# Stores of what ScalarE has just copied are begun by ScalarE in place of SyncE

## The chip, the core and the metric

The kernel runs on one core of a Trainium2 chip. The metric is the device time of one execution in microseconds (us). The engines are named as in the profile: PE is TensorE (its weight loads are shown as PEld), DVE is VectorE, ACT is ScalarE, POOL is GpSimd, SP is SyncE, which computes nothing and begins DMA transfers. SPq and ACTq are the DMA starts that SP and ACT execute. Each engine works off its own instruction list in order; they wait for each other through semaphores, and the DMA engines move data once a start has been executed.

## What is computed

One backbone layer over 512 latent tokens and 256 context tokens of width 2048, in 32-bit floats: an adaLN-modulated RMS norm, one input projection, two groups of heads that read it, a gate for each group, one output projection and a residual.

```python
def _project(xn, w_in, mu_shift):
    p = jnp.einsum('bld,de->ble', xn, w_in)
    sh, z_r, q, k, v, z_a = jnp.split(p, cuts, axis=-1)
    return _centred_shift(sh, mu_shift), z_r, q, k, v, z_a   # sh: r, k, v and two low-rank parts

def step(S, inp):                       # group A: RWKV-7 scan, both directions, 16 heads of 64
    r_t, w_t, k_t, v_t, kk_t, a_t = inp
    s_kk = jnp.einsum('bhvk,bhk->bhv', S, kk_t)
    S = (S * w_t[:, :, None, :] - s_kk[..., None] * (kk_t * a_t)[:, :, None, :]
         + v_t[..., None] * k_t[:, :, None, :])
    return S, jnp.einsum('bhvk,bhk->bhv', S, r_t)

# group B: 16 query heads on 4 key heads of 64, norm and rotary of q and k, a window of +-128
# latent tokens and all context keys in one softmax with a sink logit
# out = x + gate * (concat(y_A * silu(z_r), y_B * silu(z_a)) @ w_out)
```

## The kernel before

All matrices lie transposed: the 128 partitions are columns of the projection, the free axis is time (512 latent, then 256 context). Products in full precision are made of three with rounded halves: a weight tile from memory (`wf`) is cast by ACT to its high part (`whi`), DVE subtracts to get the low part (`wlo`), and PE multiplies high by high, high by low and low by high (`xh`, `xl` are the halves of the activations).

The 60 tiles of 128 projected columns come in kinds (`COLS`): `k`, `v`, `r` and the low-rank `lwa`, which are shifted in time, and `ak`, `av`, `q`, `zr`, `za`, which are not. The stages, by time in the trace:

- 0 to 225 us, `lockstep`: the modulation, the norm, and the first column tiles in step with the loads.
- 225 to 625: the other tiles that have context columns, beside the 8 context units of the RWKV scan.
- 625 to 1225: the tiles with latent columns only, beside 16 latent units (`unit`). Inside a unit small tiles (`it`, `iw`, `nb`) go through memory to change their layout.
- 1225 to 1362: `norms`, 12 items of norm and rotary for keys and queries (`norm_rope`), beside the last `za` tiles.
- 1362 to 1625: attention, with three quarters of the output projection beside it.
- 1625 to 1676: the last quarter; each of its 16 tiles ends in `finish`.

Four places write to memory what the next stages read. `evac` (line 988) takes a projected tile out of the accumulator: for unshifted kinds ACT copies it into `sh` and a store writes it to `dzr`, `dza`, `dq`, `dak` or `dav` (line 1031); for `k` and `r` DVE works last and the same line stores to `dk` or `dr`; for `v` PE turns it, ACT copies the turned rows back, and they are stored to `dvt` (line 1024), in two stores for a tile, latent and context. `norm_rope` ends in an ACT copy into `w`, stored to `dkf` or `dqf` (line 1468). `finish` ends in an ACT copy into `x`, stored to the output (line 735).

The order of the instructions is not that of the code. `Program` records every operation with what it reads and writes, and `order` (line 432) makes a list schedule: it keeps a clock for each engine and takes the ready operation with the longest chain of work behind it, where projection and output products and their evacuation are filler that other work precedes. Its prices for a DMA start depend on the engine: on SP a start holds the engine 450 or 625 ns and the transfers queue one behind the other, by size; on ACT it holds the engine 400 ns and what reads the result is ready 2000 ns later. `run` then emits each engine's list in that order, all from one line, which is why every row of the trace carries L500. A tile's buffer numbers are left out in the trace; tiles of different use share a buffer, so a row such as `kv<-psum` in the last stage is the `x` of `finish` in the buffer `kv`.

Of the kernel before, what the change touches and what calls it, by code (L numbers as in the profile page):

```python
# [60 lines left out]
MU_KINDS = ("lwa", "k", "v", "r")  # L61
# [451 lines left out]
class Body:  # L513
# [209 lines left out]
    def finish(self, j, acc, part):  # L723
        nc, a = self.nc, self.a
        fill, nc.fill = nc.fill, False
        y = self.t(self.wk, (128, 2, L), "fin")
        o, x = y[:, 0], y[:, 1]
        nc.sync.dma_start(out=x, in_=a["xt"][j][:, 0:L])
        nc.vector.tensor_tensor(o, acc, part, ALU.add)
        nc.vector.scalar_tensor_tensor(o, o, self.gcol[:, j:j + 1], x, ALU.mult, ALU.add)  # L730
        pt = self.t(self.pq, (128, 512), "pt", bufs=2)
        for t in range(4):
            nc.tensor.transpose(pt[:, 128 * t:128 * t + 128], o[:, 128 * t:128 * t + 128], self.ident)
        nc.scalar.copy(x, pt)
        nc.sync.dma_start(out=self.out[0].rearrange("(t p) c -> p t c", t=4)[:, :, 128 * j:128 * j + 128],
                          in_=x.rearrange("p (t c) -> p t c", t=4))
        nc.fill = fill

# [249 lines left out]
    def evac(self, j, pl, pc, o=None, banks=None):  # L988
        nc = self.nc
        kind, i, _ = COLS[j]  # L990
        segs = [(pl, 0, L)] + ([(pc, L, C)] if pc is not None else [])
        if o is None:
            o = (self.t(self.lp, (128, T), "lo", bufs=2) if kind == "lwa" else
                 self.t(self.stage, (128, T if j < NCTX else L), "sh", bufs=self.nsh))
        if kind in MU_KINDS:
            m = sum(1 for k, _, _ in COLS[:j] if k in MU_KINDS)
            om, hm = self.omm[:, m:m + 1], self.hmu[:, m:m + 1]
            for p, s, n in segs:
                nc.scalar.activation(o[:, s:s + n], p, AF.Identity, scale=om)
                nc.vector.scalar_tensor_tensor(o[:, s + 1:s + n], p[:, 0:n - 1], hm, o[:, s + 1:s + n], ALU.mult,  # L1000
                                               ALU.add)
                nc.vector.scalar_tensor_tensor(o[:, s:s + n - 1], p[:, 1:n], hm, o[:, s:s + n - 1], ALU.mult,
                                               ALU.add)
        else:
            for p, s, n in segs:
                nc.scalar.copy(o[:, s:s + n], p)
        if kind == "lwa":
            nc.scalar.activation(o[0:64, :], o[0:64, :], AF.Tanh)
            nc.sync.dma_start(out=self.dlw[i], in_=o)
            for m in range(2):  # L1010
                w = self.t(self.lp, (128, T), "lw", bufs=4)
                for h in range(2):
                    nc.sync.dma_start(out=w[64 * h:64 * h + 64], in_=self.dlw[i][64 * m:64 * m + 64])
                for st, sl in zip(self.lws[i][m], (slice(0, L), slice(L, T))):
                    nc.scalar.copy(st, w[:, sl])
                    nc.vector.tensor_tensor(st[64:128], w[64:128, sl], st[64:128].bitcast(F32), ALU.subtract)
            return
        if kind == "v":
            fill, nc.fill = nc.fill, False
            for p, (s, n) in zip(banks or (pl, pc), ((0, L), (L, C))):  # L1020
                for t in range(0, n, 128):
                    nc.tensor.transpose(p[:, t:t + 128], o[:, s + t:s + t + 128], self.ident)
                nc.scalar.copy(o[:, s:s + n], p[:, :n])
                nc.sync.dma_start(out=self.dvt[i][s:s + n].rearrange("(t q) c -> q t c", q=128),
                                  in_=o[:, s:s + n].rearrange("q (t c) -> q t c", c=128))
            nc.fill = fill
            return
        dst = {"k": self.dk, "ak": self.dak, "av": self.dav, "q": self.dq, "r": self.dr,
               "zr": self.dzr, "za": self.dza}[kind][i]
        n = T if pc is not None else L  # L1030
        nc.sync.dma_start(out=dst, in_=o[:, :n])

# [394 lines left out]
    def norm_rope(self, src, dst, tab, n, tiles, small, ps):  # L1429

        nc = self.nc
        ntt = n // 128
        x, w = (y[:, :n] for y in tiles())
        hd = lambda y: y.rearrange("p (t h c) -> p t h c", h=2, c=64)
        turn = lambda nm: self.t(ps, (128, 512), "pt", nm=nm)[:, :n]
        bc = lambda y: y.rearrange("p (t c) -> p t c", c=64).unsqueeze(2).to_broadcast([128, ntt, 2, 64])

        def turned(y, nm):
            p = turn(nm)
            for t in range(ntt):  # L1440
                nc.tensor.transpose(p[:, 128 * t:128 * t + 128], y[:, 128 * t:128 * t + 128], self.ident)
            return p

        nc.sync.dma_start(out=x, in_=src)
        pn = turned(x, "nn")
        nc.scalar.copy(x, pn)
        nc.scalar.activation(w, x, AF.Square)
        ms, *yw = (small[:, 8 * i:8 * i + 2 * ntt] for i in range(3))
        nc.vector.tensor_reduce(ms, w.rearrange("p (m c) -> p m c", c=64), AX.X, ALU.add)
        nc.vector.tensor_scalar(ms, ms, 1.0 / 64, 1e-6, ALU.mult, ALU.add)  # L1450
        inv = self.rsqrt(None, ms, 2 * ntt, yw)
        nc.vector.tensor_tensor(x.rearrange("p (m c) -> p m c", c=64), x.rearrange("p (m c) -> p m c", c=64),
                                inv.unsqueeze(2).to_broadcast([128, 2 * ntt, 64]), ALU.mult)
        if n == L:
            v = lambda y: y.rearrange("p (t h b s c) -> p t h b s c", h=2, b=2, s=2, c=16)
            sin = tab[1].rearrange("p (t b s c) -> p t b s c", b=2, s=2, c=16)
            for b in range(2):
                for q in range(2):
                    nc.vector.tensor_tensor(v(w)[:, :, :, b, q], v(x)[:, :, :, b, 1 - q],
                                            sin[:, :, b, q].unsqueeze(2).to_broadcast([128, ntt, 2, 16]), ALU.mult)  # L1460
            nc.gpsimd.tensor_tensor(hd(x), hd(x), bc(tab[0]), ALU.mult)
            nc.gpsimd.tensor_tensor(x, x, w, ALU.add)
        else:
            nc.gpsimd.tensor_tensor(hd(x), hd(x),
                                    tab[2].unsqueeze(1).unsqueeze(1).to_broadcast([128, ntt, 2, 64]), ALU.mult)
        pk = turned(x, "nk")
        nc.scalar.copy(w, pk)
        nc.sync.dma_start(out=dst, in_=w)

    def norms(self, wk, ps):  # L1470

# [242 lines left out]
```

## Time and profile before

| | before |
|---|---|
| three runs | 1673.76, 1680.74, 1681.35 us (median 1680.74) |
| profiled execution | 1677.45 us, its span 1675.6 us |
| busy share of the span | PE 93%, PEld 72%, DVE 79%, ACT 43%, POOL 24% |
| mean granted TensorE clock | 0.98 |
| DMA moved | 225.78 MB |
| DMA starts | SP 927, ACT 144 |

The span goes from the first to the last instruction of the execution. "Busy" is the time in which an engine executes; in a row of waits, `A x <- B y: total, times, longest` says that A stood still before writing x until B had written y. The DMA starts are counted in the instruction lists.

### The profile page before, as it was taken

The page shows a single profiled execution, that of the slowest core. Times are in us where ns is not written, and L with a number is a line of the kernel's source. Part 1 is how long each engine was busy: PE and PEld are TensorE (multiplying, and loading weights), DVE is VectorE, ACT ScalarE, POOL GpSimd, SP SyncE. Part 2 cuts the span into 40 slices and gives each one's busy share as a digit, 9 for nine tenths or more (in the row PEclk, how much of TensorE's full clock was granted, in tenths as well). Part 3 has the DMA queues.
Part 4 walks back from the last instruction along what each step waited for, and adds up shares of the span by engine and source line. Part 5 has one row for each costly group of instructions (what it writes and reads, how often), then busy time and mean ns, then how long its engine had stood idle before and what let it go on. Part 6 is the DMA issues. An engine that isn't in the chain of part 4 may idle for free. (4 is left out here: it accounts for less than half of the span.)

```text
span 1675.6 us, 34264 instructions
## 1 busy us (share of the span) xinstructions
PE 1556.3 (93%) x12454; PEld 1210.9 (72%) x12454; DVE 1319.0 (79%) x3921; ACT 716.6 (43%) x1484; POOL 404.0 (24%) x615
## 2 busy tenths in 40 slices
PE   7998898999999999999998898989888999999998
PEld 5666677878787777777666666767666778788887
DVE  2356889888898846989888898888889558899865
ACT  3432364333343333434443433434333338776723
POOL 2358613010111002122222323123234300111000
PEclk9999998999999999999999999999999999999999
DMA  9976464435444443333333233323343562222146
GB/s 352 332 244 227 123 196 150 129 100 148 118 145 141 139 129 125 116 89 114 107 107 100 92 106 98 100 87 111 89 133 118 170 189 76 76 70 70 45 132 195
DMA packets 215322, 225.78 MB, mean 135 GB/s; under 512 B 78704, under 2 KB 139632, under 8 KB 215152
## 3 DMA queue, kind: packets, MB, share of 16 engines
q1 hardware_dynamic: 181360, 218.86, 41.0%
q10 hardware_dynamic: 33792, 4.73, 1.7%
q8 instruction: 98, 1.61, 0.4%
q14 instruction: 72, 0.59, 0.1%
HBM read 190.49 MB, written 33.03 MB: 133 GB/s over the span
## 5 line engine op out<-in xcount | busy, mean ns | idle before, releaser
L500 PE MATMUL psum<-xh,whi.0_41_283 128*128 128x512 f32 x624 | 242.5, 412 | 1.7 <-DVE xh L500 1.1
L500 PE MATMUL psum<-xh,whi.1_44_313 128*128 128x512 f32 x624 | 240.0, 407 | 0.2 <-ACT xh L500 0.2
L500 PE MATMUL psum<-xh,wlo.0_42_287 128*128 128x512 f32 x528 | 216.3, 410 | 0.0
L500 PE MATMUL psum<-xh,wlo.1_45_325 128*128 128x512 f32 x528 | 215.2, 408 | 0.7 <-DVE wlo.1_45_325 L500 0.7
L500 PE MATMUL psum<-xl,whi.1_44_313 128*128 128x512 f32 x432 | 177.3, 411 | 4.4 <-DVE xl L500 4.4
L500 PE MATMUL psum<-xl,whi.0_41_283 128*128 128x512 f32 x432 | 177.9, 412 | 2.3 <-DVE xl L500 2.2
L500 DVE TENSOR_TENSOR s<-x,nb 128x60 f32<-128x60 f32 (+21 forms) x648 | 156.8, 242 | 10.1
L500 DVE TENSOR_TENSOR x<-x,s 128x60 f32<-128x60 f32 (+21 forms) x648 | 155.6, 240 | 10.6
L500 PEld LDWEIGHTS psum<-xh,whi.0_41_283 128*128 128x128 f32 x624 | 119.0, 192 | 29.6 <-issue 4.1
L500 PEld LDWEIGHTS psum<-xh,whi.1_44_313 128*128 128x128 f32 x624 | 117.8, 190 | 24.7 <-issue 2.9
L500 PEld LDWEIGHTS psum<-xh,wlo.0_42_287 128*128 128x128 f32 x528 | 101.3, 192 | 22.4 <-issue 1.6
L500 PEld LDWEIGHTS psum<-xh,wlo.1_45_325 128*128 128x128 f32 x528 | 100.5, 190 | 22.4 <-DVE wlo.1_45_325 L500 1.5
L500 PEld LDWEIGHTS psum<-xl,whi.0_41_283 128*128 128x128 f32 x432 | 83.4, 193 | 21.4 <-DVE xl L500 4.0
L500 PEld LDWEIGHTS psum<-xl,whi.1_44_313 128*128 128x128 f32 x432 | 82.4, 191 | 22.4 <-DVE xl L500 5.7
L500 ACT COPY uv<-psum 64x128 f32<-64x128 f32 (+2 forms) x103 | 29.1, 282 | 135.0 <-DVE uv L500 70.0
L500 PE MATMUL psum<-kr,bk 64*128 64x128 f32 (+1 forms) x640 | 67.0, 298 | 13.4 <-DVE x L500 4.5
L500 ACT ACTIVATE e<-psum,drv 128x256 f32<-128x256 f32 x96 | 44.4, 476 | 78.5 <-PE psum L500 23.1
L500 PEld LDWEIGHTS psum<-kr,bk 64*128 64x128 f32 (+1 forms) x640 | 54.0, 195 | 29.6 <-issue 10.1
L500 PE MATMUL psum<-uv,ar 64*64 64x64 f32 (+1 forms) x1280 | 71.2, 234 | 1.4 <-ACT uv L500 1.4
L500 PE MATMUL psum<-uv,kb 128*64 128x64 f32 (+1 forms) x848 | 64.9, 244 | 8.0 <-DVE uv L500 7.5
L500 PEld LDWEIGHTS psum<-uv,kb 128*64 128x64 f32 (+1 forms) x848 | 46.8, 141 | 32.5 <-DVE uv L500 13.9
L500 POOL TENSOR_TENSOR s<-s 128x128 f32<-128x128 f32 x56 | 34.8, 622 | 139.8 <-DVE s L500 111.8
(376 smaller groups left out, 3828.2 us busy)
## 6 DMA issues: line engine op xcount, KB each, us to landing
wf.0_40_230<-in_wt_dram SPq DMA_DIRECT2D x72, 256.0 KB, 2.7
wf.1_43_236<-in_wt_dram SPq DMA_DIRECT2D x72, 256.0 KB, 2.8
wf.2_50_248<-in_wt_dram SPq DMA_DIRECT2D x72, 256.0 KB, 2.8
x<-in_wga_dram SPq DMA_DIRECT2D x64, 256.0 KB, 2.8
nb<-it SPq DMA_DIRECT2D x24, 496.0 KB, 4.0
kr<-in_wss_dram SPq DMA_DIRECT2D x22, 512.0 KB, 7.1
kb<-in_wss_dram SPq DMA_DIRECT2D x22, 512.0 KB, 6.0
uv<-dvt SPq DMA_DIRECT2D x48, 128.0 KB, 2.9
```

What stands on the lines that cost most here:

```text
L500: getattr(getattr(self.nc, o.eng), o.f)(*a, **k)
```

## The change

In four places a store that SP began is begun by ACT. In `evac` the choice goes by kind: `k` and `r`, which DVE writes last, stay with SP. 72 stores move: 16 of value rows, 28 of unshifted columns (`ak` 2, `av` 2, `q` 8, `zr` 8, `za` 8), 12 of normed keys and queries, 16 of the result. ACT executes a store's start in its own list, where it waits for the end of the copy that it stores. As `order` prices starts by engine, the whole schedule is made again.

```diff
@@ finish
         nc.scalar.copy(x, pt)
-        nc.sync.dma_start(out=self.out[0].rearrange("(t p) c -> p t c", t=4)[:, :, 128 * j:128 * j + 128],
+        nc.scalar.dma_start(out=self.out[0].rearrange("(t p) c -> p t c", t=4)[:, :, 128 * j:128 * j + 128],
                           in_=x.rearrange("p (t c) -> p t c", t=4))
@@ evac
                 nc.scalar.copy(o[:, s:s + n], p[:, :n])
-                nc.sync.dma_start(out=self.dvt[i][s:s + n].rearrange("(t q) c -> q t c", q=128),
+                nc.scalar.dma_start(out=self.dvt[i][s:s + n].rearrange("(t q) c -> q t c", q=128),
                                   in_=o[:, s:s + n].rearrange("q (t c) -> q t c", c=128))
...
         n = T if pc is not None else L
-        nc.sync.dma_start(out=dst, in_=o[:, :n])
+        (nc.sync if kind in MU_KINDS else nc.scalar).dma_start(out=dst, in_=o[:, :n])
@@ norm_rope
         nc.scalar.copy(w, pk)
-        nc.sync.dma_start(out=dst, in_=w)
+        nc.scalar.dma_start(out=dst, in_=w)
```

SP's list at about 231 to 238 us of the trace, where `lockstep` hands over to the context units: `dlw` is the low-rank columns in memory, read back into `kr` and `kb`, `g`, `x` and `wf.2` are loads of weights. Before:

```order
147 L500 DMA dlw_101<-uv_47_239 128x768
148 L500 DMA kr_36_216<-dlw_100 64x768
149 L500 DMA dvt_72<-kr_33_209 128x4x128
150 L500 DMA dvt_72<-kr_33_209 128x2x128
151 L500 DMA dvt_73<-ar_32_234 128x4x128
152 L500 DMA g_256<-in_wz_dram 128x512
153 L500 DMA x_1012<-in_wga_dram 128x512
154 L500 DMA wf.2_50_248<-in_wt_dram 128x512
155 L500 DMA kb_37_219<-dlw_101 64x768
```

And after:

```order
147 L500 DMA dlw_101<-uv_47_239 128x768
148 L500 DMA kr_36_216<-dlw_100 64x768
149 L500 DMA x_1012<-in_wga_dram 128x512
150 L500 DMA wf.2_50_248<-in_wt_dram 128x512
151 L500 DMA g_256<-in_wz_dram 128x512
152 L500 DMA kb_37_219<-dlw_101 64x768 x2
153 L500 DMA kr_33_209<-dlw_101 64x768 x2
```

The three `dvt` starts are gone from SP, and the loads of weights stand in another order. ACT's list at the same place, copies of turned value rows (`kr_33`, `ar_32`) among activations and casts of the low-rank part (`uv_22`, `lwl`). Before:

```order
156 L500 COPY kr_33_209<-psum 128x512
157 L500 ACTIVATE uv_47_239<-uv_47_239 64x768
158 L500 ACTIVATE uv_30_232<-uv_30_232,s_202 128x256
159 L500 ACTIVATE nb_1114<-nb_1114,s_202 128x512
160 L500 COPY ar_32_234<-psum 128x512
161 L500 COPY kr_33_209<-psum 128x256
162 L500 CAST uv_22_950<-kr_35_214 128x256
163 L500 CAST whi.1_44_313<-wf.2_50_248 128x512
164 L500 CAST lwl_21_2064<-kr_35_214 128x512
165 L500 ACTIVATE ar_32_234<-uv_30_232,drv_271 128x256
```

And after:

```order
156 L500 COPY kr_33_209<-psum 128x512
157 L500 ACTIVATE uv_47_239<-uv_47_239 64x768
158 L500 DMA dvt_72<-kr_33_209 128x4x128
159 L500 ACTIVATE uv_30_232<-uv_30_232,s_202 128x256
160 L500 ACTIVATE nb_1114<-nb_1114,s_202 128x512
161 L500 COPY ar_32_234<-psum 128x512
162 L500 CAST whi.1_44_313<-wf.2_50_248 128x512
163 L500 COPY kr_33_209<-psum 128x256
164 L500 CAST uv_22_950<-kr_35_214 128x256
165 L500 DMA dvt_72<-kr_33_209 128x2x128
166 L500 CAST lwl_21_2068<-kr_35_214 128x512
167 L500 ACTIVATE ar_32_234<-uv_30_232,drv_271 128x256
```

Each `dvt` start stands one instruction behind its copy, and a `whi` cast has moved ahead of a copy. ACT's list in the last stage, with the `x` of `finish` in `kv`, `uv`, `bk` and `p`. Before:

```order
1383 L500 CAST whi.0_41_283<-wf.2_50_248 128x512
1384 L500 COPY kv_204<-psum 128x512
1385 L500 CAST whi.1_44_313<-wf.0_40_230 128x512
1386 L500 COPY uv_114_16123<-psum 128x512
1387 L500 COPY uv_115_16129<-psum 128x512
1388 L500 COPY bk_16136<-psum 128x512
1389 L500 COPY p_6182<-psum 128x512
```

And after:

```order
1458 L500 CAST whi.0_41_283<-wf.2_50_248 128x512
1459 L500 COPY kv_204<-psum 128x512
1460 L500 DMA out_dram<-kv_204 128x4x128
1461 L500 CAST whi.1_44_313<-wf.0_40_230 128x512
1462 L500 COPY uv_114_16104<-psum 128x512
1463 L500 DMA out_dram<-uv_114_16104 128x4x128
1464 L500 COPY uv_115_16110<-psum 128x512
1465 L500 DMA out_dram<-uv_115_16110 128x4x128
1466 L500 COPY bk_16121<-psum 128x512
1467 L500 DMA out_dram<-bk_16121 128x4x128
1468 L500 COPY p_6217<-psum 128x512
1469 L500 DMA out_dram<-p_6217 128x4x128
```

Each store stands directly behind its copy, ahead of the next cast of a weight tile.

## Rows read from the trace of the kernel before

**Rows 1.** Windows by stage: us, busy (x instructions) of PE, PEld, DVE, ACT, POOL; clock; DMA share; GB/s.

```profile
225.00:625.00 400.00, 378.52 (x3242) 308.12 (x3241) 332.35 (x1102) 158.99 (x343) 52.87 (x103) 0.98 0.48 142
625.00:1225.00 600.00, 555.98 (x5248) 415.37 (x5247) 515.74 (x1771) 236.95 (x501) 159.60 (x331) 0.98 0.35 104
1225.00:1362.00 137.00, 119.73 (x839) 89.95 (x837) 100.65 (x378) 47.41 (x87) 46.53 (x40) 0.96 0.43 142
1625.00:1676.00 51.00, 45.65 (x228) 37.18 (x226) 28.38 (x43) 16.41 (x28) 0.00 (x0) 0.99 0.61 186
```

**Rows 2.** Moved stores, by tile: duration of a start in ns (min/median/max), first and last start.

```profile
L500 SPq DMA_DIRECT2D dvt<-kr x14: 373/390/816, 233.1 to 500.3; - x14
...
L500 SPq DMA_DIRECT2D out_dram<-uv x6: 372/394/427, 1625.5 to 1667.0; - x6
...
L500 SPq DMA_DIRECT2D out_dram<-kv x2: 498/848/1197, 1643.5 to 1662.7; - x2
```

**Rows 3.** Starts that ACT executes before the change, by tile.

```profile
L500 ACTq DMA_DIRECT2D x<-iw x24: 319/466/1503, 314.7 to 1258.1; - x24
```

**Rows 4.** Waits from 225 to 1362 us: us in total, times, longest.

```profile
DVE wlo.0_42_287 L500 <- ACT whi.0_41_283 L500: 28.3, 26, 2.4
...
DVE wlo.1_45_325 L500 <- ACT whi.1_44_313 L500: 26.2, 18, 4.2
...
DVE kk L500 <- DMA x<-in_wga_dram: 13.8, 12, 2.7
...
DVE x L500 <- DMA nb<-it: 8.1, 10, 2.0
...
DVE kr L500 <- ACT kr L500: 0.2, 1, 0.2
```

**Rows 5.** Waits of SP's queue over the whole span.

```profile
SPq L500 <- ACT sh L500: 39.7, 17, 4.5
```

**Rows 6.** Timeline of SP around 235 us: start, duration, instruction.

```profile
232.06 0.53 SPq L500 DMA_DIRECT2D dlw<-uv  x1
...
233.12 1.55 SPq L500 DMA_DIRECT2D dvt<-kr  x2
...
237.50 0.45 SPq L500 DMA_DIRECT2D kb<-dlw  x1
```

**Rows 7.** Timeline of ACT at 245 us; in brackets the idle time before, and its end.

```profile
245.11 0.41 ACT L500 CAST sh<-kr 128x256 fp32r<-128x256 f32 x1 [1.72 <-DMA kr<-dlw]
245.42 0.29 ACT L500 COPY s<-s 128x128 f32<-128x128 f32 x1
246.93 0.41 ACT L500 CAST sh<-kb 128x256 fp32r<-128x256 f32 x1 [1.22 <-DMA kb<-dlw]
```

**Rows 8.** Timeline of ACT at 799 us, a DMA start and the next copy.

```profile
799.00 1.50 ACTq L500 DMA_DIRECT2D x<-iw  x1
799.26 0.26 ACT L500 COPY uv<-psum 64x128 f32<-64x128 f32 x1
```

**Rows 9.** Timelines of SP and of ACT at 1300 us.

```profile
1298.56 1.09 SPq L500 DMA_DIRECT2D kv<-dqf  x2
...
1301.92 1.05 ACT L500 CAST kr<-kv 128x1024 fp32r<-128x1024 f32 x1 [1.25 <-DMA kv<-dqf]
```

**Rows 10.** Timeline of all engines at 314 us: starts on two queues.

```profile
314.67 1.06 SPq L500 DMA_DIRECT2D rz<-iw  x1
...
314.71 1.31 ACTq L500 DMA_DIRECT2D x<-iw  x1
```

**Rows 11.** Timelines of ACT, PEld and SP in the last stage.

```profile
1656.54 0.62 ACT L500 CAST whi.1_44_313<-wf.1_43_236 128x512 fp32r<-128x512 f32 x1 [1.78 <-PE psum L500]
...
1659.52 0.42 PEld L500 LDWEIGHTS psum<-xh,whi.1_44_313 128*128 128x128 f32 x2
...
1671.91 0.59 ACT L500 COPY p<-psum 128x512 f32<-128x512 f32 x1 [1.27 <-PE psum L500]
...
1672.52 0.37 SPq L500 DMA_DIRECT2D out_dram<-p  x1
```

**Rows 12.** Window around 1247 us, columns as in rows 1.

```profile
1240.00:1254.00 14.00, 11.11 (x101) 7.88 (x101) 11.11 (x55) 4.24 (x9) 6.25 (x7) 0.88 0.45 145
```

## The prediction

> **What bounds the kernel now.** I read the busy time by stage first [rows 1]. TensorE (PE) is busy 378.5 of 400 us while the context units run, 556.0 of 600 in the latent units, 119.7 of 137 around the norms and 45.7 of 51 in the last stage; the readings between hold matmuls that are queued as filler, so what PE does not do is what it waits for. ACT is busy only 159.0, 237.0, 47.4 and 16.4 us of the same stretches. It is not the bound by its load; it can only matter where somebody waits for one of its results.
>
> Who waits for ACT is the second view [rows 4]: between 225 and 1362 us PE, PE's weight loads and DVE together waited for ACT 127 times, 104.7 us in all (30 rows with one of these in front and ACT behind; the two largest and the last are shown). The two large ones are the same thing: ACT rounds a weight tile (`whi`), DVE subtracts to get its low part (`wlo`): 28.3 us in 26 waits and 26.2 in 18. By the counts of rows 1, ACT executed 343 + 501 + 87 = 931 instructions in that stretch, so **127/931, about 14% of ACT's instructions, had somebody behind them who was already idle**. That share is my exchange rate for any delay on ACT. The waits on loads are the third reading: DVE's 13.8 us for the `wga` tiles and 8.1 for the `nb` tile [rows 4], which SP's queue starts. SP's own view shows what the change is about: its queue stood at its head 39.7 us waiting for ACT's copies into `sh` [rows 5]; but SP is not a computing engine, and a wait there costs something only if a load behind it is then late for somebody.
>
> **What is removed.** 72 DMA starts leave SP: 16 of the value rows (`dvt`), 28 of unshifted columns, 12 of normed keys and queries, 16 of the result. One took a median of 0.39 us for `dvt`, 0.39 for the result from `uv`, and up to 1.20 in one from `kv` [rows 2]; I use 0.42 as the middle, 30 us of SP's sequencer. With them go the head waits for their copies. I looked behind each for a load that somebody waited for, and found three places:
> - From 233.12 two `dvt` starts, 1.55 us together, and a third stand ahead of the `kb<-dlw` load at 237.50, which reads what a store begun at 232.06 has written [rows 6]. ACT waited 1.72 and 1.22 us for loads of `dlw` [rows 7]. Without the `dvt` starts the load goes earlier by up to these 1.55 us, if that store has landed by then; the second wait bounds the gain at 1.22, and I take 1.2.
> - Behind a `dvt` start at about 435 a `wga` load that DVE waits for: 0.5 us by the 0.39 of rows 2 and the gap to the next start.
> - At 1298.56 the loads `kv<-dqf`, behind a store of `sh`; ACT sat idle 1.25 us for them [rows 9]. The load is held by its own producer too, so I take half, 0.65 us.
>
> Together −2.35 us. All other moved starts on SP have prefetched weights behind them, which lie two or three buffers ahead of their use; I cost them at nothing, and if that cover were thinner than it looks, the gain would be the rival below.
>
> **What is added.** The same 72 starts on ACT, now each behind its own copy. ACT already starts 144 DMAs, and one of these took a median of 0.47 us and up to 1.50 [rows 3]. There the start costs ACT little: at 799.00 a start of 1.50 us ran on, and ACT's next copy was at work from 799.26 [rows 8], so start and computing overlap when the work was queued ahead. A moved store differs: in the planned order 47 of the 72 stand directly behind the copy whose result they store, 24 one instruction later, so the start has to wait for that copy to end, and everything queued behind it on ACT waits as well. The price of one is then the start, 0.42, and the overlap that back-to-back ACT instructions have and that is lost: 245.11 + 0.41 = 245.52 against a next start of 245.42, 0.10 us [rows 7]. So 0.52 us. Bounds: 0 where ACT is idle afterwards anyway, 1.5 where a start is as long as the longest of rows 3.
>
> Queued behind these stores are the casts of weight tiles (21 of the 72 stand right before a `whi` cast), `psum` copies and activations. Outside the last stage there are 56 stores: 56 × 0.52 = 29.1 us of delay, of which 14% meets an idle consumer: **+4.0 us**. At the transition near 235 ACT has a run without a pause, but ends it with waits for the `dlw` loads of 1.72 and 1.22 us [rows 7], which absorb the 3 starts there (1.6 us).
>
> **The last stage** holds 16 stores. ACT is busy 16.4 of 51 us [rows 1]. The worst place is a `whi` cast behind a store: 1656.54 + 0.62, and PE loads that tile first at 1659.52 [rows 11]; between lie 2.4 us, of which the DVE subtraction needs its share only for `wlo`, used later still. A start of 0.42 to 1.20 [rows 2] fits, so +0. At the very end the last copy runs 1671.91 to 1672.50 and SP starts the store at 1672.52 [rows 11]: the handover to another engine costs 0.02 us, so doing it on ACT **gains nothing at the tail**. If the margin were gone, 8 such casts by 0.52 would give +4.
>
> One rule of the Trainium skill speaks against a gain, its page "DMA: Bandwidth & Descriptors", section "Issuing engines are not separate DMA queues": starts given to several engines save only sequencer time, since all of them run on the same 16 DMA engines. By it the landing times don't change at all, which is what the sum above assumes with its rows.
>
> **The sum.** The profiled execution took 1677.45 us: −2.35 + 4.0 + 0 gives 1679.1. The median of the three runs lies 3.3 higher, at 1680.74, and by it the sum would be 1682.4. I take **1680**: no change that can be told.
>
> **Rivals.**
> 1. *Shorter SP line, faster.* With 30 us of starts and the head waits of rows 5 gone, `wga` and `nb` loads begin earlier. Half of 13.8 + 8.1 would be −11, which more than pays for ACT's starts where these fall into ACT's idle time: 1666.5 by the profiled execution, 1669.8 by the median, so about 1669. For: SP's queue is in order and PE is short of work just where DVE waits. Against: the `wga` load needs a buffer that DVE's previous use frees, which no earlier place in the queue brings forward.
> 2. *ACT's starts land on the path, slower.* Stores stand directly behind copies, so the casts and `psum` copies behind them are late where PE's next work needs them. If half of the 56 instead of 14% meet somebody waiting: 28 × 0.52 = +14.6, less 2.35: 1689.7 by the profiled execution, 1693.0 by the median, so about 1692. It decides from about 20 of the 56 (20 × 0.52 = 10.4, less 2.35, is +8). For: the 21 stores in front of `whi` casts, and the 44 waits of DVE for these casts [rows 4]. Against: ACT's idle time is over half of each stage [rows 1], and it mostly waits for PE.
> 3. *Starts on both queues get in each other's way.* At 314.67 SP and at 314.71 ACT began a start, and they took 1.06 and 1.31 us instead of 0.4 [rows 10]; but at 799.00 one took 1.50 by itself, with no SP start beside it [rows 8]. If starts of SP cover a quarter of the time (855 left, at 0.42 or a little more, of 1676 us), 14 of the 56 cost 0.9 us more, 14% of it awaited: +1.8, about 1682. The Trainium skill, page "Perfetto Trace Analysis", section "DMA Instruction — HWDGE (DVE, Sync)", says that two sequencers share one descriptor generator behind a lock whose wait is inside the start. Rows 10 agree, rows 8 show a long start with no partner.
> 4. *Another order.* The planner counts an ACT start otherwise than an SP one, so the whole plan is made anew. Around the units the filler moves only by a few tens of matmuls, but PE's stalls may fall elsewhere. A stall costs twice when the granted clock drops after it: over 1240 to 1254 it was 0.88 [rows 12], which at the lower level of 1.2 GHz is 3.4 us of the 14, or 1.7 us lost. Five more or fewer of these are ±8.5 us: 1671 or 1689, and with the stalls themselves past it on either side.
>
> That the change doesn't do what it says is excluded: the changed program has 216 DMA starts on ACT against 144.
>
> **Chances.** Forecast 0.44; rival 1 (faster) 0.20; rival 2 (slower) 0.16; rival 3 (same) 0.08; rival 4 0.12, half to each side. A measurement of this kernel can tell about 0.5%, 8.4 us, from no change: below 1672.3 is faster, above 1689.1 slower. Faster 0.20 + 0.06 = 0.26, same 0.44 + 0.08 = 0.52, slower 0.16 + 0.06 = 0.22. The range takes in rival 1 with some microseconds below it and rival 2 with some above: 1664 to 1696. Cases of the same sign, 1672 to 1689, hold the likeliest.
>
> **What would show it.** Right: PE busy unchanged by stage, the waits of DVE for `whi` casts up by a few microseconds and no more, the waits for `wga` and `nb` near 13.8 and 8.1, SP's head wait for `sh` gone, and the last store's start on ACT within 0.1 us of its copy's end. Rival 1: these load waits halved. Rival 2: DVE's waits for ACT's casts from 54.5 to 65 or more, with PE idle behind them. Rival 3: ACT starts of `dvt` or of the result near 1 us beside SP starts. Rival 4: stage lengths that differ in both directions and another count of slow stretches. I am wrong if a stage without moved stores, such as attention, changes by more than the others.

## The result and the profile after

The changed kernel is **slower: 1693.32 us against 1675.69**, medians of six runs each taken side by side (ratio 1.0085, 95% interval 1.0064 to 1.0106; this ratio, of the kind that every comparison below uses, is not the quotient of the two medians, which is 1.0105). The three runs shown ahead of the prediction were on the high side of what before does; with more runs its median lies at 1676 to 1679. The profiled execution took 1689.92 us, its span is 1688.0.

The windows below have the columns of [rows 1]. Their bounds are 225 us and three events that both kernels have: the first store of a `zr` tile, the first load of a `za` tile in attention, and the end; at each of the first two events PE has executed the same number of filler matmuls (2212 and 3658). Before:

```profile
225.00:639.57 414.57, 393.09 (x3306) 319.45 (x3304) 338.88 (x1112) 164.21 (x352) 56.58 (x113) 0.98 0.48 141
639.57:1363.42 723.85, 662.05 (x6024) 494.48 (x6022) 611.28 (x2140) 279.14 (x578) 202.41 (x361) 0.98 0.36 111
1363.42:1675.60 312.18, 299.15 (x1747) 247.64 (x1746) 245.04 (x470) 190.85 (x406) 30.49 (x22) 1.00 0.32 102
```

After:

```profile
225.00:649.31 424.31, 397.12 (x3301) 319.92 (x3299) 339.55 (x1110) 163.32 (x351) 52.86 (x113) 0.98 0.47 138
649.31:1376.40 727.09, 664.56 (x6024) 496.84 (x6022) 621.32 (x2140) 278.00 (x578) 196.96 (x361) 0.97 0.38 111
1376.40:1688.00 311.60, 299.50 (x1746) 249.13 (x1746) 246.17 (x470) 191.23 (x406) 30.85 (x22) 0.99 0.33 102
```

Of the 12.4 us by which the span grew, 9.7 lie beside the context units, 3.2 beside the latent units and norms, −0.6 in attention and the last stage. In the first of these PE stands still 27.2 us where it stood 21.5 (424.31 − 397.12 and 414.57 − 393.09), and is busy 4.0 longer with the same work, at the same granted clock (0.98); why it is busy longer stays open. Each window is that of one execution: e1 below, which has the order of before, differs from before by up to 3.4 us in a window, so the 3.2 and the −0.6 say little.

Now the lines that the prediction named. The waits from 225 to 1376 us, which answer to [rows 4]:

```profile
DVE wlo.1_45_325 L500 <- ACT whi.1_44_313 L500: 26.6, 21, 2.1
DVE wlo.0_42_287 L500 <- ACT whi.0_41_283 L500: 18.8, 15, 2.5
DVE kk L500 <- DMA x<-in_wga_dram: 15.7, 16, 3.5
DVE x L500 <- DMA nb<-it: 10.2, 12, 2.0
```

In these two rows DVE waits for ACT's casts 45.4 us where it waited 54.5 (a third row, of one wait, adds 1.6), and all waits of PE, its weight loads and DVE for ACT sum to 107.0 us, before to 104.7: no delay from the starts shows there. The waits for the `wga` and `nb` loads are 25.9 us against 21.9: the shorter SP list did not shorten them. SP's wait for `sh` [rows 5] is gone; the largest that are left of SP's waits for ACT are:

```profile
SPq L500 <- ACT g L500: 11.1, 3, 7.3
SPq L500 <- ACT kr L500: 10.2, 6, 3.1
```

The moved starts themselves, by tile with the columns of [rows 2]:

```profile
L500 ACTq DMA_DIRECT2D dvt<-kr x14: 366/383/427, 229.7 to 508.5; - x14
...
L500 ACTq DMA_DIRECT2D dza<-sh x8: 326/326/787, 1236.3 to 1373.3; - x8
...
L500 ACTq DMA_DIRECT2D out_dram<-uv x6: 378/378/431, 1637.9 to 1679.3; - x6
...
L500 ACTq DMA_DIRECT2D out_dram<-kv x2: 378/378/379, 1653.9 to 1673.8; - x2
```

None took more than 0.79 us; the two from `kv` that had taken 0.50 and 1.20 on SP take 0.38. How such a start lies in ACT's work is seen at the transition, the place of [rows 6, 7]:

```profile
229.11 0.59 ACT L500 COPY kr<-psum 128x512 f32<-128x512 f32 x1
229.59 0.84 ACT L500 ACTIVATE uv<-uv 64x768 f32<-64x768 f32 x1
229.73 0.43 ACTq L500 DMA_DIRECT2D dvt<-kr  x1
230.34 0.50 ACT L500 ACTIVATE uv<-uv,s 128x256 f32<-128x256 f32 x1
...
233.35 0.41 ACT L500 CAST uv<-kr 128x256 fp32r<-128x256 f32 x1
233.49 0.37 ACTq L500 DMA_DIRECT2D dvt<-kr  x1
233.89 0.62 ACT L500 CAST lwl<-kr 128x512 fp32r<-128x512 f32 x1
```

The start begins 0.03 us after its copy has ended (229.70, 229.73), while ACT already works on the instruction that stands between the copy and the start in its list. The first start is over before that instruction ends and costs nothing; the second is over 0.10 us after it, and leaves ACT idle for 0.13 us (233.76 to 233.89). Over the whole kernel 23 of the 72 starts begin while ACT works on another instruction. Only 14 of the 72 have an instruction of ACT beginning within 0.15 us behind their end, and in 3 more one begins before the end; behind the others ACT was idle or still at work.

And the tail:

```profile
1684.27 0.59 ACT L500 COPY p<-psum 128x512 f32<-128x512 f32 x1 [1.27 <-PE psum L500]
1684.88 0.38 ACTq L500 DMA_DIRECT2D out_dram<-p  x1
```

The copy ends at 1684.86 and the store starts 0.02 us later, as on SP [rows 11]. From the first store of the result to the last it takes 46.98 us, before 46.97.

So every local line stands where a cheap or free move would leave it, and yet the kernel lost 14 us by the ratio, 18 by the medians. What is left is the order.

### The profile page after: what moved, and what is told of

It is laid out like the page before. It is cut to its first block, busy times and chain, and to the rows that moved or that the text cites. A ratio compares the mean times of both kernels' runs of the same rounds, so it can differ in the third digit from the quotient of the medians.

```text
span 1688.0 us, 34253 instructions
## 1 busy us (share of the span) xinstructions
PE 1562.1 (93%) x12454; PEld 1214.5 (72%) x12454; DVE 1332.2 (79%) x3921; ACT 716.0 (42%) x1484; POOL 395.1 (23%) x615
## 5 line engine op out<-in xcount | busy, mean ns | idle before, releaser
L500 DVE TENSOR_TENSOR x<-x,s 128x60 f32<-128x60 f32 (+21 forms) x648 | 160.5, 248 | 10.0
L500 PE MATMUL psum<-kr,bk 64*128 64x128 f32 (+1 forms) x640 | 69.4, 295 | 14.6 <-DVE bk L500 7.1
```

What stands on the lines that cost most here:

```text
L500: getattr(getattr(self.nc, o.eng), o.f)(*a, **k)
```

## The experiments

Two theories: **S**, the starts on ACT cost the time; **P**, the new plan does, whoever executes the starts. `Program` lets them be told apart, since the engine for which an instruction is planned and the engine to which it is given at the end can be made different: a keyword `emit` is kept with the operation, and only `run` reads it.

```diff
+        o.emit = k.pop("emit", eng)
...
-                getattr(getattr(self.nc, o.eng), o.f)(*a, **k)
+                getattr(getattr(self.nc, o.emit), o.f)(*a, **k)
```

**e1: order of before, starts on ACT** (one of the four places is shown here and for e2).

```diff
-        nc.sync.dma_start(out=dst, in_=w)
+        nc.sync.dma_start(out=dst, in_=w, emit="scalar")
```

> All 72 stores are planned as SP's, so that the order of every instruction is that of before, and only at the end are these starts given to ACT's list, at the place in the common order where SP would have had them. Theory S (the starts on ACT delay what stands behind them there): the change's loss shows here, 1685 to 1697 us, and DVE's and PE's waits for ACT grow by 10 us or more. Theory P (the new plan is the loss, the starts are cheap): within 4 us of before, 1672 to 1680 us.

Measured: 1675.88 us, ratio **1.0001** (0.9976 to 1.0025). The waits of PE, its weight loads and DVE for ACT sum to 103.2 us, where theory S wanted 10 or more above 104.7.

**e2: order of the changed kernel, starts on SP.**

```diff
-        nc.scalar.dma_start(out=dst, in_=w)
+        nc.scalar.dma_start(out=dst, in_=w, emit="sync")
```

> The reverse: the 72 stores are planned as ACT's, so that the order of every instruction is that of the changed kernel, and only their starts go back to SP's list, at the same place in the common order. Theory P: as slow as the changed kernel, 1686 to 1697 us, with the loss in the context units (the sixth to seventh nb load 10 us or more later than before). Theory S: as before, 1672 to 1680 us.

Measured: 1695.34 us, ratio **1.0112** (1.0085 to 1.0139). Its windows lose at the same places:

```profile
225.00:652.35 427.35, 400.28 (x3300) 322.73 (x3298) 338.66 (x1109) 162.79 (x350) 52.47 (x113) 0.97 0.47 137
652.35:1379.00 726.65, 661.79 (x6024) 495.92 (x6022) 623.26 (x2140) 277.50 (x578) 197.66 (x361) 0.98 0.37 111
1379.00:1692.00 313.00, 298.79 (x1746) 247.76 (x1746) 246.34 (x470) 190.61 (x406) 31.28 (x22) 1.00 0.34 102
```

while those of e1 are those of before within 3.4 us:

```profile
225.00:642.44 417.44, 394.37 (x3304) 319.73 (x3302) 339.06 (x1111) 163.44 (x352) 55.40 (x113) 0.98 0.48 140
642.44:1362.86 720.42, 659.54 (x6022) 493.74 (x6021) 611.65 (x2139) 278.52 (x578) 199.87 (x361) 0.98 0.38 111
1362.86:1675.30 312.44, 300.28 (x1749) 249.33 (x1748) 246.00 (x471) 190.19 (x406) 30.45 (x22) 0.99 0.33 103
```

With either order, moving the 72 starts between the queues is worth nothing that can be measured: with the old order ACT's starts are 0.0001 dearer, with the new one 0.0027 cheaper (1.0085 against 1.0112), within intervals of 0.0021 to 0.0027 to each side. One place differs all the same: from the first store of the result to the last it takes 48.91 us in e2, with SP's starts in the new order, and 46.98 in the changed kernel. Going from one order to the other costs all of the loss. Theory S falls. The runs agree with what the Trainium skill states on its page "DMA: Bandwidth & Descriptors", section "Issuing engines are not separate DMA queues": spreading starts over engines saves sequencer time alone, and in e1 the time that SP was spared shortened nothing (1.0001).

**e3, e4: a new plan without the change.** Is the lost time special to this plan, or does any new plan lose?

```diff
-    AFTER = {"vector": 127, "scalar": 131, "gpsimd": 76, "tensor": 196, "sync": 905}
+    AFTER = {"vector": 128, "scalar": 131, "gpsimd": 76, "tensor": 196, "sync": 905}
```

> No store moves. One latency in the planner, after DVE, goes from 127 to 128 ns: a change without meaning for the chip that makes the plan anew to about the same extent as the change does. Theory P: a plan made anew differs by several microseconds, 1678 to 1696 us. Theory S: the plan as such costs nothing, within 4 us of before, 1672 to 1680 us.

> The same in the other direction, 127 to 126 ns. Theory P: again off by several microseconds and not by the same as with 128, 1678 to 1696 us. Theory S: within 4 us of before, 1672 to 1680 us.

Measured: e3 1.0061 (1.0038 to 1.0085), e4 1.0032 (1.0005 to 1.0058). One nanosecond in a table of the planner, with no store moved, costs 10 and 5 us. A new plan as such can cost that much. The constants in that table may be ones with which the plan happens to run well; how they were chosen is not on record.

**e5, e6: parts of the change.**

> Only the 16 stores of value rows are planned and begun by ACT. The plan first differs at the transition near 225 us, where the changed kernel's does, and PE's list by less than half as many lines as with the whole change. If the loss of the changed kernel comes from what the value rows' stores move around the context units: 1684 to 1696 us, with the sixth to seventh nb load 10 us late. If each new plan is its own draw: anywhere from 1672 to 1692, and not the changed kernel's stage by stage. If starts alone counted: 1676 to 1678.

> Only the 28 stores of unshifted columns are planned and begun by ACT; PE's list differs from before by about as much as with the whole change. If the loss has one place in the columns' stores: as slow as the changed kernel, 1686 to 1697, and then e5 is near before. If each new plan is its own draw: 1674 to 1692, whatever e5 gives, so that the losses of e5 and e6 don't add to the whole change's 17 us.

Measured: value rows alone 1.0031 (1.0014 to 1.0047), unshifted columns alone 1.0001 (0.998 to 1.0023). They don't add to 1.0085, and the columns, whose plan differs from before nearly as far as the whole change's, lose nothing. Neither group of stores carries the loss.

**e7, e8: the change with another draw**, a draw being a plan whose time is a matter of chance. The edit of e4 (126) and of e3 (128) on the changed kernel.

> The whole change, and the planner's latency after DVE at 126 in place of 127 ns. If the loss belongs to the change (its prices for starts on ACT make worse plans): 1688 to 1700 us, as the changed kernel. If the changed plan is one draw among many: off from the changed kernel's 1693 by 4 us or more, most likely lower, 1676 to 1689.

> The same with 128 ns. If the loss belongs to the change: 1688 to 1700 us. If a draw: 1676 to 1689 and another time than with 126.

Measured: e7 1.0103 (1.0079 to 1.0127), e8 1.0071 (1.0047 to 1.0095). Both are about as slow as the changed kernel, which speaks against a plain draw: three plans of the change, all of them above the two of e3 and e4. The margins are uneven, though: with 126 the change adds 0.0071 to e4, with 128 only 0.0010 to e3, which is within the intervals, and e8's median lies 1.5 us above the range that its expectation gave a draw. That a part of the loss belongs to the change is likely from these.

**e9, e10, e13: the change with its stores priced.** What does the planner believe of a store on ACT? That it holds ACT for 400 ns, that readers have it 2000 ns later, and that it is not in the queue of transfers, into which SP's stores go with their size. 72 transfers vanish from the plan's queue, but not from the chip. Theory Q says that the loss comes from this price, theory D that each plan is a draw whatever the price. Here the transfers go back into the queue:

```diff
+            if store:
+                x = outs[0]
+                o.move = max(180, math.prod(x.shape) * 4 / (360 if int(x.ap[-1][1]) >= 128 else 240))
...
                 free[e] = o.end = o.at + o.dur
+                if o.move:
+                    o.end = moved = max(moved, free[e] + 650) + o.move
...
-                              2000 * (e == "scalar" and o.f == "dma_start"))
+                              2000 * (e == "scalar" and o.f == "dma_start" and not o.move))
```

Two things change beside the queue and the 2000 ns: with its size a store also gets a longer chain of work behind it, by which `order` ranks operations, and what reads it is ready by ACT's latency (131 ns) behind the transfer, where a store on SP has 905.

> The whole change, but in the planner the 72 stores begun by ACT join the one queue of transfers with their size, as SP's do, in place of a flat 2000 ns for their readers. Theory Q (the changed plans are worse as a kind, since the planner believes 72 transfers to be off its queue): the loss goes, 1676 to 1684 us. Theory D (each plan is a draw that has nothing to do with these prices): as likely as not between 1682 and 1697 us.

> The same, with the planner's latency after DVE at 128 ns, for a second plan of this kind. Theory Q: 1676 to 1686 us, some 6 us or more below the change with 128 (ratio 1.0071). Theory D: 1682 to 1697 us.

> Third plan of the priced kind, with 126 ns. Theory Q: 1.000 to 1.006, and below the unpriced plan with 126 (1.0103) by at least 0.004. Theory D: as likely above 1.006 as below.

Measured: 1.0050 (1.0034 to 1.0067), 1.0025 (1.0004 to 1.0045), 1.0063 (1.0041 to 1.0084). The first is at the upper end of what theory Q wanted and inside what theory D gave (1683.64 us, in 1682 to 1697), the second in Q's range alone, the third just beyond Q's; but each lies below the unpriced plan with the same constant, by 0.0035, 0.0046 and 0.0040. Only the second comes near before.

**e14, e15: more plans without the change**, by the latency after SP (905 to 910) and after POOL (76 to 78).

> No store moves; the planner's latency after an SP transfer is 910 in place of 905 ns. A third new plan of the kernel before: by those with 126 and 128 (1.0032, 1.0061) 1.000 to 1.007. Theory D wants one of the plans of this kind to reach the changed kernel's 1.008 or more.

> The same with the latency after POOL at 78 in place of 76 ns: 1.000 to 1.007; Theory D as in the run before.

Measured: 1.0002 (0.9983 to 1.0021) and 1.0040 (1.0020 to 1.0061). All plans by kind, as ratios to before:

| kind of plan | ratios | mean |
|---|---|---|
| before, made anew (e3, e4, e14, e15) | 1.0061, 1.0032, 1.0002, 1.0040 | 1.0034 |
| change, stores in the plan's queue (e9, e10, e13) | 1.0050, 1.0025, 1.0063 | 1.0046 |
| change as it is (after, e8, e7) | 1.0085, 1.0071, 1.0103 | 1.0086 |

The priced plans lie among those that were only made anew, but for e13 just above them; the unpriced ones lie above all seven others, the nearest pair by 0.0008. By these means some **6 us (0.0034) is what a new plan cost against the one in use**, 0 to 10 in single plans, and some 9 (0.0086 − 0.0034), of which the pricing takes back 7, comes with the planner's price for a store on ACT. With three plans of a kind this is likely rather than settled, and which part of the price does it, the missing queue, the flat 2000 ns or the rank, was not tried.

Two things weaken it. Compared line by line in the traces (PE's instructions in order, by tile and shape), e4, e14 and e15 have only some 1800 to 3100 of PE's 12454 instructions in another order than before, the changed kernel some 5400; e3, with some 5300, is the slowest of its kind. So the smaller loss of the first kind may in part be the smaller distance; the priced plans (4800 to 5800) are as far from before as the unpriced ones (4300 to 5700), and that comparison stands. And e6 has 28 stores with the unpriced start, differs from before in some 4700 places and loses nothing, so the price does not always cost.

**e11, e12, e16: the parts that hardly touch the plan**, norms, result, both.

> Only the 12 stores of normed keys and queries are planned and begun by ACT; the plan differs from before in few lines, behind 1235 us. The changed kernel lost 7 us between the last context-free unit and attention. If the norms' stores do that: 1682 to 1688 us. If that loss was brought by the plan of what runs beside the norms: 1674 to 1681 us.

> Only the 16 stores of the result are planned and begun by ACT; PE's list is that of before, word for word. Starts in front of the casts of the last stage cost nothing and save nothing at the tail: ratio 0.997 to 1.003, last stage from the first store of the result to the last 46.9 to 47.1 us. If they delay the casts there: 4 us or more above before.

> The stores of norms and of the result alone are planned and begun by ACT. The parts gave 0.9996 and 0.9984; together 0.996 to 1.001. If the gain of the result's part was no more than scatter: 0.999 to 1.001.

Measured: 0.9996 (0.9980 to 1.0011), 0.9984 (0.9968 to 1.0000), 0.9987 (0.9963 to 1.0010). The norms' stores by themselves bring no loss; what the changed kernel loses beside the norms is left to the plan of the rest. In e12 PE's list is that of before word for word, and from the first store of the result to the last it takes 47.0 us:

```profile
L501 ACTq DMA_DIRECT2D out_dram<-uv x6: 378/378/443, 1621.1 to 1662.6; - x6
L501 ACTq DMA_DIRECT2D out_dram<-p x5: 378/378/422, 1630.3 to 1668.1; - x5
```

The stage that the edit concerns is as long as before, so the 0.0016 of e12 is not a gain of that stage: at 1621.1 its profiled execution was already 4.4 us ahead, by a stretch that the edit doesn't touch. None of the three is clear of before (e12's interval ends at 1.0000). No version here is shown to beat it.

## Why the prediction was wrong

The forecast of no change was made of two sums, one for SP and one for ACT, and a base. Their balance, +1.65, was about right (e1 has the starts alone within 4 us of nothing); a term that was not in them, the new order, was the whole result.

- **What is removed, −2.35: hardly seen.** ACT's waits for `dlw` at the transition were 1.72 and 1.22 us; after the change it waits for these loads three times:

```profile
236.89 0.41 ACT L500 CAST uv<-kr 128x256 fp32r<-128x256 f32 x1 [1.97 <-DMA kr<-dlw]
...
241.57 0.41 ACT L500 CAST sh<-kb 128x256 fp32r<-128x256 f32 x1 [0.83 <-DMA kb<-dlw]
...
243.98 0.41 ACT L500 CAST sh<-kr 128x256 fp32r<-128x256 f32 x1 [1.08 <-DMA kr<-dlw]
```

  together 3.88 us against 2.94. There the work in between stands in another order. e1, with the order of before, shows what the start's move alone does:

```profile
233.73 0.40 ACT L501 CAST uv<-kr 128x256 fp32r<-128x256 f32 x1 [0.48 <-DMA kr<-dlw]
...
245.06 0.41 ACT L501 CAST sh<-kr 128x256 fp32r<-128x256 f32 x1 [1.91 <-DMA kr<-dlw]
```

  together 2.39, which is 0.55 less than before where I had taken 1.2. The wait for the `kb` load is gone, as forecast; a part of it came back at the other two places.
- **What is added, +4.0: too high.** I priced every start at 0.52 us of delay. In the trace of after only 14 of the 72 have work of ACT right behind their end, which they delay by about their 0.36 us; at 14% awaited that is an estimated 0.7 us. e1 bounds starts gained and lost together at −4 to +4 us, e2 agrees. The mechanism, that a start waits for its own copy and holds up what is behind it, is there; mostly nothing was ready behind it, or it ran beneath the instruction between the two.
- **The last stage and the tail, 0: right**, 46.97 us before, 46.98 after, 47.0 in e12; the handover costs 0.02 us on either engine.
- **Rival 1 (loads earlier): refuted** by 25.9 us of waits where half of 21.9 was its mark, and more cleanly by e1, where SP's list is as short and the order that of before: 14.6 and 8.9, together 23.5 us. **Rival 2 (starts on the path): refuted**, though its time, 1692, was the one measured: its mark was DVE's waits for casts at 65 us or more, and they fell to 45.4 (47.0 with the third row); e2 has the loss without a single moved start on ACT. A time that fits is no proof of its mechanism.
- **Rival 3 (starts in each other's way): not what cost the time.** In the changed kernel no moved start took more than 0.79 us, and that one, at 1263.42, had no start of SP beside it. In e1 one reached the rival's mark, beside a start of SP, and ACT's next cast came 0.75 us later for it:

```profile
234.03 0.34 SPq L501 DMA_DIRECT2D g<-in_wz_dram  x1
...
234.19 1.18 ACTq L501 DMA_DIRECT2D dvt<-ar  x1
235.41 0.62 ACT L501 CAST lwl<-kr 128x512 fp32r<-128x512 f32 x1 [0.75 <-issue]
```

  The lock that the Trainium skill describes (page "Perfetto Trace Analysis", section "DMA Instruction — HWDGE (DVE, Sync)") may be in that start, but no run shows it: SP's start was over at 234.37, ACT's at 235.37. e1 as a whole is not slower for it.
- **Rival 4 (another order): what happened.** Two steps of it failed. I gave it 12%, on the reading that the filler moves by only a few tens of matmuls around each unit; but the same small counts go with the full loss (at the first store of a `zr` tile the counts are equal to the matmul, and 9.7 us are gone). And I gave it **half to each side**. Of the seven plans of the first two kinds in the table above none was faster than before, and six were slower by 0.25 to 0.63% with intervals clear of 1. That reads as if the plan in use stood at the good end of its neighbours, so that a step from there mostly goes down; why it does is argued, not shown. The two prices for a start, one inside the plan's queue of transfers and one outside, stood in the description of the kernel. I used them only to say that the order would change, and did not ask in which direction the plan would err. The price of its stalls, a clock that drops behind them, was not the loss: the mean granted clock is 0.980 in both profiled executions.
- **The base:** the three runs of before had a median of 1680.74, three more lay at 1674.79 to 1676.30. The 0.9 us that I added to the sum for that median had no ground, but changes nothing.

Where inside the plan the 9.7 us beside the context units go is only partly seen. One piece shows how an order makes a wait: PE's waits for one result of ACT within a unit, the copy into `q`, from 225 us to the first store of a `zr` tile. Before, and e1 (the same order, starts on ACT):

```profile
PEld psum L500 <- ACT q L500: 1.2, 4, 0.4
```

```profile
PEld psum L501 <- ACT q L501: 1.2, 4, 0.4
```

After, and e2 (the same order, starts on SP):

```profile
PEld psum L500 <- ACT q L500: 6.7, 7, 2.9
...
PE psum L500 <- ACT q L500: 4.0, 2, 2.4
```

```profile
PEld psum L501 <- ACT q L501: 6.2, 7, 2.9
PE psum L501 <- ACT q L501: 3.5, 2, 2.4
```

The wait follows the order and not the engine of the starts. It is not the common cause, though. e7, the slowest plan, has 1.8 us of it, and loses 10.5 us in the same stretch all the same:

```profile
225.00:650.11 425.11, 398.05 (x3304) 319.70 (x3302) 340.86 (x1111) 162.70 (x352) 53.44 (x113) 0.98 0.47 138
650.11:1387.37 737.26, 675.42 (x6024) 507.36 (x6022) 615.55 (x2140) 278.00 (x578) 200.09 (x361) 0.96 0.37 109
```

In the second stretch e7 loses 13.4 us more, and there it is not waiting: PE stands still 61.8 us as before, and is busy 13.4 longer with the same 6024 instructions, at a granted clock of 0.96 where before had 0.98. What is lost beside the context units is many waits in places that differ from plan to plan; a common cause of them inside the plans was not found.

## What to carry to other kernels

In a kernel whose order comes from a planner, an edit has two effects, and they can be measured apart: plan the instruction as before and give it to the new engine only at the end, and the reverse. Before crediting or blaming an edit, make the plan anew once or twice with a constant changed by nothing; here that alone moved the time by 0.0 to 0.6%, where the change under test moved it by 0.85%. And when an instruction changes its engine, look at what the planner believes of it there: here the plans in which 72 transfers were still on the chip but no longer in the plan's queue were likely worse as a kind.

## What was not expected of the hardware

A start on ACT that stands one instruction behind its copy does not wait for the instruction between the two to end: it began 0.03 us after the copy's end while that one was running. 23 of the 72 began beneath another instruction in this way. The 72 starts took a median of 0.36 us on ACT and 0.38 on SP, 26.7 us together against 29.9; single ones are long on either engine, 1.18 us on ACT in e1 and 1.20 on SP before. And one and the same kernel, e1, took from 1664.09 to 1683.99 us in ten runs, at mean granted clocks of 0.992 and 0.976 in those two: the scatter between runs is as large as the effect that was looked for, and in these ten the slower runs mostly have the lower clock.
